# Queries and keys of three attention groups by seven products of halves, with one addition per weight sum

## The chip, the core and the metric

The kernel runs on one core of a Trainium2 chip. The time is the device time of one execution in microseconds (us), measured on the chip; the kernel before took 2248.38, 2249.28 and 2249.44 us in three runs (median 2249.28 us). The smallest change that a measurement of this kernel can tell from none is about 0.2%, some 4.5 us.

The engines are called by short names. PE is the matrix engine, PEld its loading of stationary operands. DVE is the vector engine, ACT the engine for activation functions and scaled copies, POOL the general engine whose queue also issues some transfers, and SP the engine that only issues transfers. Each works through a queue of its own in order, and they wait for each other by semaphores.

## The reference, cut to what matters

Two layers of a transformer over 256 tokens of width 2048, in float32. Each layer is a mixer (differential attention in the first, latent attention in the second), an attention over 256 memory tokens and an MLP with squared ReLU of inner width 8192; each of the three begins with an RMS norm and is added to the residual stream. The change touches the first mixer most, and the MLP a little:

```
def diff_attention(h, wqkv, lam_vecs, subln, wo, cos, sin, lambda_init):
    q, k, v = jnp.split(h @ wqkv, 3, axis=-1)          # h: 256 x 2048, wqkv: 2048 x 6144
    q = partial_rope(q.reshape(B, S, 2 * DA_HEADS, DA_HEAD_DIM), cos, sin, DA_ROT)
    k = partial_rope(k.reshape(B, S, 2 * DA_HEADS, DA_HEAD_DIM), cos, sin, DA_ROT)
    ...
        p = jax.nn.softmax(s, axis=-1)
        a = (p[:, :, 0] - lam * p[:, :, 1]).astype(v.dtype)
        return jnp.einsum('bhqk,bkhd->bqhd', a, v)
    o = rms_norm(o, subln) * (1.0 - lambda_init)
    return o.reshape(B, S, D_MODEL) @ wo

def sq_relu_mlp(h, wup, wdown):
    return jnp.square(jax.nn.relu(h @ wup)) @ wdown
```

## The kernel before

**Arithmetic.** Every float32 operand is split into a high and a low part, and each product is computed as high times high, high times low and low times high: three 128x512 matmuls where one would do. A weight arrives as a raw tile of 1 MB (128x2048: four blocks of 128 inputs by 512 outputs). Per half of it (128x1024), ACT casts the high part `whi` (L193) and DVE subtracts it from the raw values to give `wlo` (L194); PE then does 12 matmuls with the half. A raw tile is called a job below; it has two halves and 24 matmuls, and `matmul_chunk` (L241) does four of them for 512 outputs. Activations are kept transposed, as tiles `unit` with both parts of 512 features by 256 tokens.

**Order of work.** The list `plan` names all jobs in the order in which PE uses them, and `fill` keeps four of them ahead (L205). There are six raw tiles, so SP issues a load when an earlier job has been split, and four buffers each of `whi` and `wlo`, so that splitting runs at most four halves ahead of PE. Between the halves `pump` lets small tasks take their turn on PE (transposes, scores, the steps of an attention), so that the chains of softmax and normalization on DVE, ACT and POOL run while PE does jobs. PE's order is that of the program; the order of the other engines' queues comes from the scheduler of the framework, except where `keep_in_program_order` ties an instruction.

**Differential attention.** It has four groups of two heads with 512 outputs each of query, key and value. `project_diff` (L1157) does the three chunks of a group, twelve jobs: `heads_T` (L461) evacuates queries and keys to a tile `ev` (L443), POOL rotates the first quarter of each head with the tables `cos` and `sin` (`rope`, L446 to L459, six small instructions per 128 tokens), PE transposes the result against `identr` and ACT and DVE split it; `values` (L482) evacuates the values. While the attention of one group (`attend_diff`, L615) takes its turns, PE does the output projection of the group before (four `da_wo` jobs) and the twelve jobs of the next group. DVE's part of an attention are the maxima `nmax`, the reciprocals `rsum`, the weighted differences `a` of two softmaxes (L631, L632), the low parts of transposed probabilities (`raw` from `ax`, L514) and the norm of the heads. The tables are computed once, with a sine on ACT for `sin` (L955) and, after a few DVE steps on the angle that use its result, for `cos` (L959).

**Seven products.** Seven of the eight blocks of each MLP already use a form of Strassen's scheme (class `Seven`, L723): both the tokens and the pair (input half, output half) of the weight are split in two, and seven products p1 to p7 of sums of blocks, two jobs each (x = 0, 1), take the place of eight. Sums of activations s1 to s4 come from class `Forms` (L368). Sums of weights are made in place in the raw tiles: p5 adds a freshly loaded tile to that of p1, and p7 adds the same tile to that of p3, on DVE, in two additions of 128x1024 (L760), each just ahead of the split of that half; p6 and p4 come from tiles to which the next block is added by an accumulating transfer on POOL's queue (L765). Seven's jobs stand between other jobs of the MLP (`pr` are its banks, `mm` those of the others). Sums of products end in 128x512 additions on DVE (L794).

Of the kernel before, what the change touches and what calls it, by code (L numbers as in the profile page):

```python
# [17 lines left out]
P = 128  # L18
# [27 lines left out]
def trunk(ctx, tc, x, xT, mem, memT, positions, gcols, gfinal, lam_vecs, consts, W, out):  # L46
# [321 lines left out]
    class Forms(Stream):  # L368
# [11 lines left out]

        def halves(self, key, x, src):
# [20 lines left out]
        def sums(self):  # L402
# [3 lines left out]
            for x in range(2):  # L406
                a11, a12, a21, a22 = (self.raw[t][:, 8 * h + 4 * x : 8 * h + 4 * x + 4] for t in range(NT) for h in range(2))
                for key, o, p, q, op in (
                    ("s1", a22, a21, a22, ALU.subtract), ("s3", a21, a11, a21, ALU.subtract),
                    ("s2", a22, a22, a11, ALU.subtract), ("s4", a12, a12, a22, ALU.add),  # L410
                ):
                    nc.vector.tensor_tensor(o, p, q, op)
                    self.halves(key, x, o)
                yield T_TURN

# [8 lines left out]
        def unit_of(self, u):  # L424
            return FormUnit(self, u)

# [188 lines left out]
    def attend_diff(q, k, v, dst, coef, subcols):  # L615


        def block(t, heads, out):
# [17 lines left out]
            yield T_TURN  # L636
            if not out:
                out.append((yield from side_bank()))
            po = out[0]
            nb = nk // P  # L640
            for i, h in enumerate(heads):
                for kb in range(nb):
# [3 lines left out]
                        val(v, 0, kb, h * S, S), val(v, 1, kb, h * S, S), kb == 0, kb == nb - 1,  # L646
# [76 lines left out]
    class Seven:  # L723
# [20 lines left out]
        def job(self, p, x):  # L744
            def run():
# [11 lines left out]
                for h in range(2):  # L757
                    if other is not None:
                        half = slice(2 * h * CH, 2 * (h + 1) * CH)
                        nc.vector.tensor_tensor(o[:, half], o[:, half], other[:, half], ALU.add)  # L760
# [13 lines left out]
        def products(self, a, u, copied, out):  # L774
            p, x = u
            form = a.form(self.A[p])
            need(form.tasks)
# [4 lines left out]
            for h, (hi, lo) in enumerate(take()):  # L782
                for k in range(2):
                    kk = 4 * x + 2 * h + k
                    wh, wl = (w[:, k * CH : (k + 1) * CH] for w in (hi, lo))
                    mmul(o, form[:, 0, kk], wh, kk == 0 and not onto, False, not onto)
                    mmul(o, form[:, 0, kk], wl, False, False, not onto)
                    mmul(o, form[:, 1, kk], wh, False, kk == 7, not onto)
# [618 lines left out]
```

## Time and profile before

| | |
|---|---|
| runs before, median | 2249.28 us |
| the profiled execution | 2248.09 us, of which its span is 2246.3 us |
| PE busy | 2221.8 us of the span (99%) |
| DVE busy | 1683.7 us (75%) |
| ACT busy | 1366.9 us (61%) |
| POOL busy | 154.0 us (7%) |
| moved | 484.10 MB, 216 GB/s mean |
| differential attention with its four groups | about the first 360 us |
| the two MLPs' seven products | about 560 to 1080 and 1620 to 2150 us |

The times of the engines are those in which an instruction runs; PE's matmuls overlap, each 128x512 lasts 0.39 us and the next starts before it ends. A row of the timeline has the start in us, the duration in us, engine, line, operation, output and inputs with the buffer numbers left out, shapes and a count; in brackets stands how long the engine had been idle and who ended that. A row of the waits has engine and line, what it waited for, the sum in us, the count and the longest. A row of the windows gives a stretch of time and each engine's busy time in it, the number of its instructions in brackets, then PE's granted clock, the share of the transfer engines and GB/s.

### The profile page before, as it was taken

How to read it: one execution, taken by the hardware profiler on the slowest of the kernel's cores; microseconds unless marked ns; L12 is line 12 of the kernel's file. 1: busy time of each engine (PE TensorE's matmuls, PEld its weight loads, DVE VectorE, ACT ScalarE, POOL GpSimd, SP SyncE). 2: the span in 40 equal slices, each digit the busy share in tenths (PEclk: the TensorE clock that was granted, in tenths of full speed). 3: DMA queues.
4: the chain of work that ended last, by engine and by line, in shares of the span. 5: the costliest groups of instructions: out<-in, count | busy, mean ns of one | idle time of the engine just before them, and what ended most of it. 6: DMA issues, size and time to landing. Idle time of an engine off the chain costs nothing.

```text
span 2246.3 us, 27519 instructions
## 1 busy us (share of the span) xinstructions
PE 2221.8 (99%) x10521; PEld 1853.4 (83%) x10521; DVE 1683.7 (75%) x1892; ACT 1366.9 (61%) x1815; POOL 154.0 (7%) x250
## 2 busy tenths in 40 slices
PE   9999999999999999999999999999999999999998
PEld 7888888888888888888889888888888888888886
DVE  6665647778878788788765766778887887887864
ACT  7544645666666666666655655566666666666664
POOL 0201010000000000000000311000000000000001
PEclk9999999999999999999999999999999999999999
DMA  9446555436887887887955334643689788788682
GB/s 364 168 135 219 193 192 200 162 124 221 245 273 230 243 269 236 243 262 225 282 177 181 111 141 151 243 150 133 238 250 264 237 246 261 238 245 262 231 299 75
DMA packets 73717, 484.10 MB, mean 216 GB/s; under 512 B 8432, under 2 KB 8816, under 8 KB 18032
## 3 DMA queue, kind: packets, MB, share of 16 engines
q1 hardware_dynamic: 64944, 422.56, 52.1%
q0 software_dynamic: 8064, 58.72, 13.7%
q8 instruction: 82, 1.34, 0.2%
q10 hardware_dynamic: 576, 1.05, 0.2%
q14 instruction: 51, 0.42, 0.1%
HBM read 480.20 MB, written 2.10 MB: 215 GB/s over the span
## 4 chain that ended last, share of the span: by engine, by line
PE 92%; DVE 5%; ACT 1%; DMA 0%; issue 0%; ACTq 0%; POOLq 0%
PE mm L155 66%; PE pr L155 21%; PE ax L155 3%; DVE raw L760 2%; DVE wlo L194 2%; PE ax L159 2%; PE mm L159 1%; ACT whi L193 1%; DMA raw<-in_da_wqkv_dram 0%; DVE unit L289 0%; DVE x L438 0%; DVE unit L316 0%; DVE unit L487 0%; DVE os L658 0%; ACT unit L571 0%
## 5 line engine op out<-in xcount | busy, mean ns | idle before, releaser
L194 DVE TENSOR_TENSOR wlo<-raw,whi 128x1024 fp32r<-128x1024 f32 (+2 forms) x962 | 1161.3, 1212 | 470.2 <-ACT whi L193 430.6
L193 ACT CAST whi<-raw 128x1024 fp32r<-128x1024 f32 (+2 forms) x962 | 1002.1, 1042 | 742.9 <-PE mm L155 583.0
L155 PE MATMUL mm<-whi,unit 128*128 128x512 f32 (+3 forms) x4544 | 1442.1, 389 | 1.5 <-ACT unit L571 0.9
L155 PEld LDWEIGHTS mm<-whi,unit 128*128 128x128 f32 x4544 | 849.1, 188 | 168.0 <-ACT unit L315 1.5
L155 PE MATMUL mm<-wlo,unit 128*128 128x512 f32 (+3 forms) x2272 | 877.1, 386 | 11.8 <-DVE wlo L194 11.8
L155 PEld LDWEIGHTS mm<-wlo,unit 128*128 128x128 f32 x2272 | 427.4, 188 | 95.5 <-DVE wlo L194 17.2
L155 PE MATMUL pr<-whi,unit 128*128 128x512 f32 x1568 | 501.9, 390 | 0.0
L155 PEld LDWEIGHTS pr<-whi,unit 128*128 128x128 f32 x1568 | 294.4, 188 | 61.0
L155 PE MATMUL pr<-wlo,unit 128*128 128x512 f32 x784 | 305.0, 389 | 0.0
L155 PEld LDWEIGHTS pr<-wlo,unit 128*128 128x128 f32 x784 | 147.2, 188 | 30.3
L760 DVE TENSOR_TENSOR raw<-raw,raw 128x1024 f32<-128x1024 f32 x112 | 133.5, 1219 | 0.9 <-DMA raw<-in_mlp_wup_dram 0.7
L765 POOL DMA_DIRECT2D raw<-in_mlp_wup_dram x56 | 49.4, 882 | 1126.4 <-DVE wlo L194 1126.4
L438 DVE TENSOR_TENSOR x<-x,mm 128x512 f32<-128x512 f32 x152 | 99.8, 681 | 9.4 <-PE mm L155 8.9
L328 POOL TENSOR_TENSOR rs<-rs,mhalf 128x1 f32<-128x1 f32 (+1 forms) x28 | 23.5, 845 | 679.8 <-DVE rs L327 679.8
L288 ACT CAST unit<-ax 128x512 fp32r<-128x512 f32 (+1 forms) x88 | 49.0, 568 | 26.1 <-PE ax L159 23.6
L289 DVE TENSOR_TENSOR unit<-ax,unit 128x512 fp32r<-128x512 f32 (+1 forms) x88 | 57.4, 661 | 3.4 <-ACT unit L288 1.3
L500 ACT ACTIVATE p<-ax,nmax 128x256 f32<-128x256 f32 (+1 forms) x80 | 33.7, 429 | 30.0 <-DVE nmax L498 29.5
L322 ACT ACTIVATE junk<-x 128x512 bf16<-128x512 f32 x56 | 35.2, 628 | 9.4 <-DVE x L438 8.4
L155 PE MATMUL ax<-unit,unit 128*128 128x256 f32 (+1 forms) x240 | 37.2, 281 | 0.0
L155 PEld LDWEIGHTS ax<-unit,unit 128*128 128x128 f32 x240 | 34.4, 190 | 2.5
L155 PE MATMUL ax<-raw,unit 128*128 128x256 f32 (+1 forms) x240 | 35.3, 279 | 0.8 <-ACT unit L486 0.6
L155 PEld LDWEIGHTS ax<-raw,unit 128*128 128x128 f32 x240 | 32.0, 190 | 2.4 <-ACT unit L486 1.0
(150 smaller groups left out, 925.5 us busy)
## 6 DMA issues: line engine op xcount, KB each, us to landing
raw<-in_mlp_wup_dram SPq DMA_DIRECT2D x128, 1024.0 KB, 5.0
raw<-in_mlp_wdown_dram SPq DMA_DIRECT2D x128, 1024.0 KB, 5.3
raw<-in_mlp_wup_dram POOLq DMA_DIRECT2D x56, 1024.0 KB, 9.5
raw<-in_da_wqkv_dram SPq DMA_DIRECT2D x45, 1024.0 KB, 5.0
raw<-in_da_wo_dram SPq DMA_DIRECT2D x16, 1024.0 KB, 5.0
raw<-in_ca_wkv_dram SPq DMA_DIRECT2D x16, 1024.0 KB, 5.0
raw<-in_mla_wo_dram SPq DMA_DIRECT2D x16, 1024.0 KB, 5.2
raw<-in_ca_wq_dram SPq DMA_DIRECT2D x8, 1024.0 KB, 4.9
```

Of the source, the lines that this page charges most:

```text
L155: return nc.tensor.matmul(o, stationary, moving, start=start, stop=stop, skip_group_check=not alone)
L159: nc.tensor.transpose(o, src, ident)
L193: nc.scalar.copy(hi, r)
L194: nc.vector.tensor_tensor(lo, r, f32(hi), ALU.subtract)
L288: nc.scalar.copy(hi, src)
L289: nc.vector.tensor_tensor(dst[:, 1, :n, t * P : (t + 1) * P], src, f32(hi), ALU.subtract)
L322: nc.scalar.activation(junk[:, : src.shape[1]], src, AF.Square, accum_out=acc)
L328: nc.gpsimd.tensor_tensor(r[:, :n], r[:, :n], mhalf.broadcast_to([P, n]), ALU.pow)
L438: nc.vector.tensor_tensor(xc, xc, ps, ALU.add)
L500: nc.scalar.activation(pr[:, i * w : (i + 1) * w], sb[:, i * w : (i + 1) * w], AF.Exp, bias=nmax[:, i : i + 1], accum_out=ssum[:, i : i + 1],)
L760: nc.vector.tensor_tensor(o[:, half], o[:, half], other[:, half], ALU.add)
L765: add = nc.gpsimd.dma_start(o, self.source(*block, x), accum_op=ALU.add)
```

## The change

**Queries and keys of groups 1, 2 and 3** are computed by `Seven`, which now takes the name of any weight and a first chunk. The two output halves are the 512 queries and the 512 keys of the group, the two input halves are those of the 2048 features, and the two token halves the two tiles of 128 tokens. A job of `Seven` feeds one output bank of 128 tokens, so its half has six matmuls and the job twelve: 14 jobs take the place of the group's eight jobs of 24. Each group's p5 and p7 need four weight sums on DVE and its p6 and p4 four accumulating transfers on POOL's queue.

**The sums of activations** come from the new class `GivenForms`: SP loads the transposed input once more (2 MB, into two raw tiles), ACT multiplies it by the norm's gain, DVE makes the sums and ACT and DVE split them, into four units. This happens once, behind the query chunk of group 0.

**The order of the jobs** is set by `diff_line`: the 14 jobs are laid between eight others, the output projection of the group before (for the first line the values of group 0) and the values of the next group. So the attention of group 0 begins before its own values exist, and it now waits for them (`while not v()`). Rotated queries and keys (`rotated_T`) wait until the attention before has given its units free.

**The weight sums**, in the groups and in the MLPs alike, are now one addition of 128x2048 each (L787), ahead of both splits of the job, and tied to the program's order; before there were two of 128x1024, one ahead of each split, which the scheduler placed. The number of free banks for side tasks is one lower while the lines run.

```diff
+    class GivenForms(Forms):
+        def __init__(self, src, units, gcol):
+            self.src, self.units, self.gcol = src, units, gcol
+            self.forms = {}
+            task = Task(self.sums())
+            for key in ("s1", "s2", "s3", "s4"):
+                self.form(key).tasks.append(task)
+
+        def sums(self):
+            for x in range(2):
+                rows = raw_tile().rearrange("p (k t) -> p k t", t=S)
+                for h in range(2):
+                    u = 2 * h + x
+                    load(rows[:, 4 * h : 4 * h + 4], self.src[:, 4 * u : 4 * u + 4, :])
+                    for i in range(4):
+                        row = rows[:, 4 * h + i]
+                        nc.scalar.activation(row, row, AF.Copy, scale=g[:, self.gcol + 4 * u + i : self.gcol + 4 * u + i + 1])
+                    yield T_TURN
+                self.sums_of(x, *(rows[:, 4 * h : 4 * h + 4, t * P : (t + 1) * P] for t in range(NT) for h in range(2)))
+                yield T_SM
+
+        def pieces(self, key):
+            if key in self.forms:
+                return super().pieces(key)
+            t, h = key
+            return [], lambda half, kk: self.units[2 * h + kk // 4].get(half, kk % 4, t)
 
...
             yield T_TURN
+            while not v():
+                yield 0.5
...
-    plan_k("da_wqkv", 24)
-    for gi in range(1, 4):
-        plan_rows("da_wo", gi - 1)
-        if gi < 3:
-            plan_k("da_wqkv", 12, start=12 * (gi + 1))
-    plan_k("ca_wkv0", 4)
-    plan_rows("da_wo", 3)
...
-        def __init__(self, l, b):
-            self.l, self.b = l, b
+        def __init__(self, name, chunk, b=None):
...
         def source(self, i, j, x):
-            return W[f"mlp_wup{self.l}"][4 * (2 * self.b + j) + 2 * i + x]
+            return W[self.name][4 * (self.chunk + j) + 2 * i + x]
...
                 split = split_pieces(o, 4 * CH, 2)
-                for h in range(2):
-                    if other is not None:
-                        half = slice(2 * h * CH, 2 * (h + 1) * CH)
-                        nc.vector.tensor_tensor(o[:, half], o[:, half], other[:, half], ALU.add)
+                if other is not None:
+                    tc.keep_in_program_order(nc.vector.tensor_tensor(o, o, other, ALU.add))
+                for _ in range(2):
                     split.next()
...
+                    mmul(o, form(0, kk), wh, kk == 0 and not onto, False, not onto)
+                    mmul(o, form(0, kk), wl, False, False, not onto)
+                    mmul(o, form(1, kk), wh, False, kk == 7, not onto)
...
+    def diff_line(gi):
+        values_of = lambda g: [("da_wqkv", 12 * g + 8 + u, CH) for u in range(4)]
+        others = values_of(0) if gi == 0 else [("da_wo", 4 * c + gi - 1, CH) for c in range(4)]
+        others = [Item(None, None, [job]) for job in others + values_of(gi + 1)]
+        seven = Seven("da_wqkv", 3 * (gi + 1)).items()
+        line = []
+        for n in (2, 1, 1, 1, 0, 2, 1) if gi == 0 else (1, 1, 1, 1, 1, 2, 1):
+            line += seven[:2] + others[:n]
+            del seven[:2], others[:n]
+        return line
+
+    diff_lines = [diff_line(gi) for gi in range(3)]
+    plan_k("da_wqkv", 8)
+    for line in diff_lines:
+        plan.extend(j for item in line for j in item.jobs)
+    plan_rows("da_wo", 2)
+    plan_k("ca_wkv0", 4)
+    plan_rows("da_wo", 3)
...
+    def chunk_steps(units_in, finish):
+        n = len(units_in)
+        ps = [bank("mm") for _ in range(NT)]
+        for u, act in enumerate(units_in):
+            need(act.tasks)
+            for h, (hi, lo) in enumerate(take()):
+                for t in range(NT):
+                    unit_part(ps[t], act, h, hi, lo, t, u == 0, u == n - 1)
+            if u == n - 1:
+                finish(ps)
+            yield
+
...
+    def rotated_T(src, r, t, i, dst, free):
+
+
+        nc.scalar.activation(r, src, AF.Copy, scale=da_scales[i][t])
+        rope(r.rearrange("p (h d) -> p h d", h=4), *rotation(t))
+
+        def task():
+            yield T_ROT
+            while not free():
+                yield 0.5
+            b = yield from side_bank()
+            split(dst, t, transpose4(r, b))
+            give_back()
+            yield T_TURN
+
+        dst.run(task())
...
+    q, k = Held(unit()), Held(unit())
+    for i, dst in enumerate((q, k)):
+            heads_T(ps[t], t, lambda i=i, t=t: da_scales[i][t], dst, rotation(t), given=lambda: da_scales)
+        if i == 0:
+            forms = GivenForms(xT, acts, G_ATTN)
+    v, before, copied = [], None, {}
+    free_banks[0] -= 1
+    for gi, line in enumerate(diff_lines):
+        o = attend_group(q, k, v)
+        nq, nk, nv = Held(unit()), Held(unit()), []
+        other = value_steps(v) if gi == 0 else output_steps(before)
+        other_then = value_steps(nv)
+
+        def produced(t, c, src, r, o=o, pair=(nq, nk)):
+            rotated_T(src, r, t, c, pair[c], lambda: all(task.done for task in o.tasks))
+
+        for item in line:
+            if item.of is not None:
+                item.of.products(forms, item.u, copied, produced)
+            elif next(other, 0) == 0:
+                next(other_then)
+        assert next(other_then, 0) == 0
+        if gi == 1:
+            mem_norm()
+        q, k, v, before = nq, nk, nv, o
```

In counts, PE's 128x512 matmuls of the projections fall by 72 (three groups, each from 192 to 168). The sums on DVE change from 112 of 128x1024 to 68 of 128x2048, the splits from 926 to 962, and POOL's queue gets 12 more accumulating transfers of 1 MB.

Three places in the queues follow. The first is ACT's queue at the tables of the rotation, just before the first rotated queries are needed. Before:

```order
L193 CAST whi_414<-raw_412 128x1024
L443 ACTIVATE ev_491<-mm_210,rq_442 128x512
L955 ACT_TABLE_LOAD
L955 ACTIVATE sin<-ang 128x96
L443 ACTIVATE ev_589<-mm_370,r_83_444 128x512
L193 CAST whi_418<-raw_412 128x1024
L443 ACTIVATE ev_601<-mm_371,r_84_446 128x512
L959 ACTIVATE cos<-ang 128x96
```
After, where `raw_563` is the second tile of the input loaded again, `unit_375` to `unit_378` are the four sums, L478 is the evacuation and `p_134_712<-pr_665` copies the first product:

```order
L478 ACTIVATE ev_638<-mm_379,r_87_470 128x512
L478 ACTIVATE ev_650<-mm_380,r_88_472 128x512
L830 COPY p_134_712<-pr_665 128x512
L193 CAST whi_594<-raw_592 128x1024
L193 CAST whi_598<-raw_592 128x1024
L388 CAST unit_375<-raw_563 128x512
L388 CAST unit_377<-raw_563 128x512
L1002 ACT_TABLE_LOAD
L1002 ACTIVATE sin<-ang 128x96
L388 CAST unit_376<-raw_563 128x512
L1006 ACTIVATE cos<-ang 128x96
L388 CAST unit_378<-raw_563 128x512
```
The sine now stands behind the copy of the first product, two casts and two high parts of the sums, and another high part stands between sine and cosine.

The second is DVE's queue in the MLP, from p4's last splits to the first of p5. Before, `wlo_7175` and `wlo_7179` belong to p4, the two tiles of p5 are `raw_7042` (x = 0) and `raw_7077` (x = 1), and `raw_7194` is the job that PE does just before p5:

```order
L194 TENSOR_TENSOR wlo_7175<-raw_6734,whi_7174 128x1024
L760 TENSOR_TENSOR raw_7042<-raw_7042,raw_7220 128x1024 x2
L194 TENSOR_TENSOR wlo_7179<-raw_6734,whi_7178 128x1024
L760 TENSOR_TENSOR raw_7077<-raw_7077,raw_7271 128x1024 x2
L289 TENSOR_TENSOR unit_7125<-ax_7263,unit_7125 128x4x128
L194 TENSOR_TENSOR wlo_7197<-raw_7194,whi_7196 128x1024
L194 TENSOR_TENSOR wlo_7201<-raw_7194,whi_7200 128x1024
L194 TENSOR_TENSOR wlo_7224<-raw_7042,whi_7223 128x1024
L794 TENSOR_TENSOR u_1381_7121<-pr_7270,u_1381_7121 128x512
```
After, at another block of the same kind: p5's tiles are `raw_5294` (x = 0) and `raw_5329` (x = 1), and `raw_5446` is the job just before p5:

```order
L194 TENSOR_TENSOR wlo_5427<-raw_4984,whi_5426 128x1024
L194 TENSOR_TENSOR wlo_5431<-raw_4984,whi_5430 128x1024
L289 TENSOR_TENSOR unit_5377<-ax_5514,unit_5377 128x4x128
L787 TENSOR_TENSOR raw_5329<-raw_5329,raw_5522 128x2048
L194 TENSOR_TENSOR wlo_5449<-raw_5446,whi_5448 128x1024
L194 TENSOR_TENSOR wlo_5453<-raw_5446,whi_5452 128x1024
L787 TENSOR_TENSOR raw_5294<-raw_5294,raw_5472 128x2048
L822 TENSOR_TENSOR u_1105_5373<-pr_5521,u_1105_5373 128x512
L194 TENSOR_TENSOR wlo_5476<-raw_5294,whi_5475 128x1024
```
Before, both sums stand ahead of the splits of the job in front of p5; after, the sum for x = 1 stands ahead of these splits, and that for x = 0 behind them.

The third is DVE's queue in the attention of group 0, from the maximum of the third score tile (`ax_904` before, `ax_984` after) to its weighted difference (`a_922` before, `a_1002` after). Before:

```order
L498 TENSOR_REDUCE nmax_913<-ax_904 128x2
L194 TENSOR_TENSOR wlo_736<-raw_729,whi_735 128x1024
L514 TENSOR_TENSOR raw_927<-ax_807,raw_927 128x256
L505 RECIPROCAL rsum_919<-ssum_914 128x2
L625 TENSOR_TENSOR rsum_919<-rsum_919,coef 128x2
L631 TENSOR_SCALAR a_922<-p_915,rsum_919 128x256
L632 SCALAR_TENSOR_TENSOR a_922<-p_915,rsum_919,a_922 128x256
```
After, the last twelve rows of that way:

```order
L194 TENSOR_TENSOR wlo_921<-raw_797,whi_920 128x1024
L540 RECIPROCAL rsum_999<-ssum_994 128x2
L522 SCALAR_TENSOR_TENSOR unit_1049<-mm_714,r_87_470,unit_1049 128x512
L194 TENSOR_TENSOR wlo_925<-raw_797,whi_924 128x1024
L660 TENSOR_TENSOR rsum_999<-rsum_999,coef 128x2
L522 SCALAR_TENSOR_TENSOR unit_1049<-mm_715,r_88_472,unit_1049 128x512
L549 TENSOR_TENSOR raw_1046<-ax_935,raw_1046 128x256
L194 TENSOR_TENSOR wlo_965<-raw_962,whi_964 128x1024
L666 TENSOR_SCALAR a_1002<-p_995,rsum_999 128x256
L327 TENSOR_SCALAR rs_1083<-ss_205_1078 128x2
L194 TENSOR_TENSOR wlo_969<-raw_962,whi_968 128x1024
L667 SCALAR_TENSOR_TENSOR a_1002<-p_995,rsum_999,a_1002 128x256
```
Before, one split stands between maximum and difference; after, four stand in these twelve rows alone, and with them the evacuation of the values of group 0 (`unit_1049`), which before was done when the attention began.

More of the change, by code (lines that the diff above doesn't have):

```diff
@@ L1177, in trunk @@
+    free_banks[0] += 1
+    o = attend_group(q, k, v)
+    m = []
+    project_group(before, each=lambda c: m.append(given_unit(memT, c, G_MEM)))
+    mk = mem_keys(m)
+    norm = Stream(G_CROSS)
+    project_group(o, norm)
     norm = cross(0, norm, m, mk)
```

64 lines of the change are left out of this document (34 added, 30 removed).

## The prediction

> **What bounds the kernel now.** I read the page first, then the windows over the groups of the differential attention and over an MLP, then what PE waited for, and last the timelines at the places that the change moves. The page's first lines:
>
> ```profile
> span 2246.3 us, 27519 instructions
> PE 2221.8 (99%) x10521; PEld 1853.4 (83%) x10521; DVE 1683.7 (75%) x1892; ACT 1366.9 (61%) x1815; POOL 154.0 (7%) x250
> ```
>
> The profiled execution took 2248.09 us, 1.8 us outside its span, and 1.2 us less than the median of the runs, 2249.28. I make the sum against 2248.1 and add 1.2 at the end. The windows of groups 1 to 3 of the attention and of one MLP stretch (PE, PEld, DVE, ACT, POOL busy):
>
> ```profile
> 82.00:172.00 90.00, 90.00 (x446) 75.76 (x446) 56.64 (x86) 47.34 (x89) 10.84 (x26) 1.00 0.44 152
> 172.00:263.00 91.00, 90.89 (x434) 75.91 (x432) 53.86 (x70) 49.00 (x79) 10.58 (x28) 1.00 0.57 197
> 263.00:354.00 91.00, 91.00 (x434) 76.12 (x433) 54.21 (x68) 44.49 (x68) 9.48 (x26) 1.00 0.54 185
> 700.00:1000.00 300.00, 296.26 (x1327) 243.94 (x1327) 247.66 (x229) 190.24 (x202) 12.31 (x14) 1.00 0.81 247
> ```
>
> PE never stands still in the attention, and DVE has a third of that time free. In the MLP DVE is at 83% and PE loses 1.2%. What PE waited for from 60 to 420 us was one row, and from 420 us to the end almost one cause:
>
> ```profile
> PE ax L159 <- DVE os L658: 0.3, 1, 0.3
> ```
>
> ```profile
> PE mm L155 <- DVE wlo L194: 11.2, 12, 0.9
> ```
>
> So a matmul less is time less, as long as DVE, which the change loads, stays ahead of PE.
>
> **Matmuls removed.** PE in the attention repeats three matmuls (high, low, low) in 0.68 us:
>
> ```profile
> 114.45 0.39 PE L155 MATMUL mm<-wlo,unit 128*128 128x512 f32 x1
> 115.13 0.39 PE L155 MATMUL mm<-wlo,unit 128*128 128x512 f32 x1
> ```
>
> 0.68 / 3 = 0.2275 us a piece; 72 fewer give 16.4 us. They are in the middle of a busy PE, so all of it counts.
>
> **MLP sums.** The twelve waits are one per block, where p5 begins (six of the seven blocks of each MLP). One of them on PE, and DVE's rows ahead of it:
>
> ```profile
> 788.22 0.39 PE L155 MATMUL pr<-whi,unit 128*128 128x512 f32 x1
> 788.45 0.39 PE L155 MATMUL mm<-whi,unit 128*128 128x512 f32 x1
> 789.77 0.50 PE L155 MATMUL mm<-wlo,unit 128*128 128x512 f32 x1 [0.93 <-DVE wlo L194]
> ```
>
> ```profile
> 781.08 1.22 DVE L194 TENSOR_TENSOR wlo<-raw,whi 128x1024 fp32r<-128x1024 f32 x1 [1.17 <-ACT whi L193]
> 782.22 2.35 DVE L760 TENSOR_TENSOR raw<-raw,raw 128x1024 f32<-128x1024 f32 x2
> 784.49 1.22 DVE L194 TENSOR_TENSOR wlo<-raw,whi 128x1024 fp32r<-128x1024 f32 x1
> 785.63 2.35 DVE L760 TENSOR_TENSOR raw<-raw,raw 128x1024 f32<-128x1024 f32 x2
> 787.90 0.68 DVE L289 TENSOR_TENSOR unit<-ax,unit 128x512 fp32r<-128x512 f32 x1
> 788.50 3.48 DVE L194 TENSOR_TENSOR wlo<-raw,whi 128x1024 fp32r<-128x1024 f32 x3
> ```
>
> PE goes on 1.32 us after 788.45 where 0.23 is usual: 1.09 lost, since two pairs of sums (2.35 each) stand ahead of the job's split, which starts at 788.50. In the new order one sum goes ahead and one behind. I replay this block. A sum of 128x2048 is not in the trace; its nearest row is the pair, 2.35, and since pair and following split start 2.27 apart I take 2.25 (bounds 2.1 and 2.4). A split in a row costs (3.48 - 1.22) / 2 = 1.13. The unit's low part waits for its high part on ACT:
>
> ```profile
> 783.67 0.58 ACT L288 CAST unit<-ax 128x512 fp32r<-128x512 f32 x1
> 788.65 1.04 ACT L193 CAST whi<-raw 128x1024 fp32r<-128x1024 f32 x1 [0.26 <-PE pr L155]
> ```
>
> Low part 784.25 to 784.9, sum x=1 to 787.1, two splits to 788.3 and 789.4 (PE wants the first at 788.45 + 0.23 = 788.7), sum x=0 to 791.6, the cast of the sum on ACT 1.05 to 792.7, its split to 793.85. PE wants that after 24 matmuls and one, at 794.1. So both margins are 0.3 to 0.4 us. The sum for x=1 also needs its transfer:
>
> ```profile
> 776.42 3.05 SPq L165 DMA_DIRECT2D raw<-in_mlp_wup_dram  x2
> ```
>
> ```profile
> DMA to landing us min/median/max: 4.7/5.5/13.3
> ```
>
> The second issue of the two ends that row and so starts at 779.1; 5.5 later is 784.6, just before 784.9. I count a third of the blocks late by 0.4, 0.13 on average: 12 x (1.09 - 0.13) = 11.6 us gained; the bounds are 13.1 and nothing.
>
> **Group 0: the tables.** Rows of ACT around sine and cosine, POOL's first rotations, and PE's transposes of them:
>
> ```profile
> 51.70 1.28 ACT L955 ACT_TABLE_LOAD   x1
> 52.99 0.28 ACT L955 ACTIVATE sin<-ang 128x96 f32<-128x96 f32 x1
> 55.27 0.28 ACT L959 ACTIVATE cos<-ang 128x96 f32<-128x96 f32 x1
> ```
>
> ```profile
> 55.62 0.61 POOL L454 TENSOR_TENSOR rope<-ev,cos 128x64 f32<-128x64 f32 x1 [1.59 <-ACT cos L959]
> 58.01 0.32 POOL L454 TENSOR_TENSOR rope<-ev,cos 128x64 f32<-128x64 f32 x1
> 60.81 0.32 POOL L454 TENSOR_TENSOR rope<-ev,cos 128x64 f32<-128x64 f32 x1
> ```
>
> ```profile
> 60.73 1.03 PE L159 MATMUL mm<-identr,ev 128*128 128x128 f32 x8
> ```
>
> After the change the same number of 128x512 matmuls, 241, stands ahead of these transposes, so PE comes to them at 60.7 again. But in ACT's queue the sine now stands behind the copy of product p1, whose last matmul is 12 matmuls, 2.7 us, ahead of the transposes: 58.0. The pieces are the copy, two casts and two high parts, with these rows for the copy and a high part:
>
> ```profile
> 777.76 0.57 ACT L802 COPY p<-pr 128x512 f32<-128x512 f32 x1
> ```
>
> 58.2 + 0.6 + 2 x 0.95 (casts in a row) + 2 x 0.58 = 61.8; table load to 63.1; sine to 63.4; the three DVE steps on the angle, with a sum of forms between them, about 1.1; cosine at 64.5, 9.2 us later than 55.27. POOL then needs 2.4 us for the first and 2.8 for the second tile, as its rows show, and had 0.4 to spare for the second. So PE waits 9.2 - 0.4 = 8.8 us, in two pieces of about 6.4 and 2.4. Nothing hides this: PE's queue is in order, and all attention stands behind.
>
> **Group 0: the attention.** While PE waits, DVE's queue waits too, since the low parts of the transposed queries stand in it. From the end of the second score tile to the transposes of the third difference PE needed this long:
>
> ```profile
> 85.39 0.22 PE L155 MATMUL ax<-maskr,identr 128*128 128x128 f32 x1
> ```
>
> ```profile
> 100.74 0.38 PE L159 MATMUL ax<-identr,a 128*128 128x128 f32 x2
> ```
>
> 15.2 us, with 54 matmuls of 128x512, and 54 stand there after the change. DVE's queue in that stretch then has eight splits (8 x 1.13 = 9.1), a sum (2.25), the pair of values (1.3) and the attention's own instructions (4.5): 17.2, and 0.4 until it can start: 2.4 us late. Group 0 together is 11.2 (6 if half of the tables' delay is made up, 16 at most).
>
> **Groups 1 to 3.** Per group DVE gets 12 splits (13.6), four sums (9.0) and five additions of products (3.0): 54.9 + 25.6 = 80.5 in a group of 90.7 - 5.5 = 85.2. That fits, but with 5 us free where 36 were, and it is late where PE waits for an instruction of the attention behind sums. Where the low part of the probabilities was just in time:
>
> ```profile
> 103.33 0.42 DVE L514 TENSOR_TENSOR raw<-ax,raw 128x256 fp32r<-128x256 f32 x1
> ```
>
> ```profile
> 104.15 0.88 PE L155 MATMUL ax<-unit,raw 128*128 128x256 f32 x6
> ```
>
> it had 0.4 us to spare; in groups 1 and 2 two sums of p7 stand shortly ahead of it, 4.5 us less that 0.4, or 3.9 with what DVE does ahead of time meanwhile. Group 3 has no seven products behind it: 0.3. Together 8.1; the bounds are nothing and two such places per group, 16. The new waits are 11.2 + 8.1 = 19.3 us.
>
> **Taken at nothing:** the second load of the input (2 MB) and 12 MB more of weights, because the transfer engines are at 44 to 57% in the groups (if that cover went, a job would cost its landing, 5.5 against PE's 5.5); the scaling and halving of the sums on ACT, beyond their place ahead of the sine; POOL's 12 issues of 0.9 us beside its 10 us per group; one free bank less (1 us either way).
>
> **Sum.** 2248.1 - 16.4 - 11.6 + 19.3 = 2239.4; with 1.2 for the median, 2240.6 us.
>
> **A rule of the skill.** The warm-up of PE in the trace took 5.45 us for 13 matmuls of 128x512, 0.43 each, against 0.2275 later, and the granted clock in the windows above is 1.00:
>
> ```profile
> 1.23 5.45 PE L905 MATMUL ax<-blank 128*128 128x512 bf16 x13 [1.23 <-DVE blank L902]
> ```
>
> If PE fell back to this after group 0's wait of 6.4 and stayed there as long as at the start, it would lose 5.45 - 13 x 0.2275 = 2.5 us. The Trainium skill ("TensorE: Matmul & The Clock Gate", section "What's actually happening") says that this is what happens after an idle window of about 3.4 us. No wait of PE in the trace, after the start, is over 1.3 us, so no run shows it yet.
>
> **Rivals.**
> - *The clock falls in group 0* as just said: 2243.1. Chance 0.12, given the forecast's waits.
> - *The sums in the MLP only move*: the margins of 0.3 us are gone, because the transfer lands later than 5.5 or the sum takes 2.4, and PE waits another 1.1 somewhere in the block. For it: the longest landing, 13.3, and DVE's 83%. Then -16.4 + 19.3 = +2.9: 2252.2. Chance 0.18.
> - *The cover holds*: DVE uses the wait in group 0 to get ahead, and the rows behind the sums are early: new waits 9, all from the tables. -19: 2230.3. Against it, the order puts sums ahead of rows that are awaited. Chance 0.15.
> - *DVE becomes the bound of the three groups* (slower): of the 36 us per group in which DVE stood idle, mostly for casts that wait for PE to free a buffer, more than 5 remain. Group time is then DVE's 80.5 plus the idle time; the change loses when the groups give back 16.4 + 11.6 + 4.5 - 11.2 = 21.3, 7.1 each, so from 11.8 us idle on. At 14, a group takes 9.3 more: -28.0 + 11.2 + 27.9 = +11.1, or 2260.4. For it: DVE must be ahead of PE but may run only four halves ahead. Against: it was never late before. Chance 0.15.
>
> That the change does less than it says is excluded by PE's queue, which has the 72 matmuls fewer.
>
> **How the numbers follow.** The forecast has 0.40, its own range is 2233 to 2247 (new waits 13 to 26, MLP gain 9 to 13). 0.2% of 2249.3 is 4.5 us, about what a measurement of this kernel can tell; faster means under 2244.8. Faster: 0.34 of the forecast, 0.08 of the clock's case, 0.15 of the cover's: 0.57. Within: 0.06, 0.04 and 0.14 of the sums' case: 0.24. Slower: 0.04 of the sums' case and 0.15 of DVE's: 0.19. For eight in ten I leave out the lower half of the cover's case and the upper half of DVE's: 2230 to 2257.
>
> **What would show it.** Right: PE's row that waits for `wlo` in the MLP shrinks from 11.2 to under 3; a wait of 6 us and one of 2.4 at the transposes near 61 us, cosine near 64.5; PE waits in groups 1 and 2 of a few us for `raw` and `a`; group periods of about 89. Wrong: the twelve MLP waits are still there, or sit elsewhere in the block; no wait at 61 us; a group that takes over 92 us with DVE at over 85; PE's pitch other than 0.2275.

## The result and the profile after

The changed kernel takes 2261.57 us (median of six runs, 2258.68 to 2263.68), the kernel before in the same rounds 2248.98 us: a ratio of 1.0058, 95% interval 1.0047 to 1.0068. It is 12.6 us slower where 8.7 us less was forecast. The profiled execution took 2263.42 us, 1.9 above the median, with a span of 2261.6.

The page's first lines, as for the kernel before:

```profile
span 2261.6 us, 27542 instructions
PE 2218.6 (98%) x10449; PEld 1843.1 (81%) x10449; DVE 1758.3 (78%) x1915; ACT 1402.9 (62%) x1881; POOL 185.1 (8%) x262
```

PE's instructions are 72 fewer, and its busy time hardly falls. The windows of the stretch in which the changed groups lie, and the MLP stretch:

```profile
60.00:120.00 60.00, 46.65 (x218) 38.23 (x216) 48.22 (x68) 38.20 (x66) 13.30 (x27) 0.86 0.47 154
160.00:260.00 100.00, 96.97 (x460) 79.82 (x459) 87.80 (x103) 64.53 (x98) 21.67 (x32) 1.00 0.73 233
260.00:360.00 100.00, 96.50 (x452) 79.79 (x451) 85.52 (x106) 65.74 (x101) 23.41 (x37) 0.98 0.73 234
700.00:1000.00 300.00, 298.66 (x1337) 244.63 (x1336) 247.07 (x218) 190.12 (x210) 10.45 (x12) 1.00 0.75 246
```

PE was fully busy in all of the attention before; now it stands still for 22% of the first row and 3% of the next two, and in the first its granted clock is 0.86. The main rows of what PE waited for up to 420 us, and from there on:

```profile
PE mm L159 <- POOL ev L494: 12.4, 2, 11.8
PE ax L155 <- DVE raw L549: 4.0, 2, 2.2
PE ax L159 <- DVE a L667: 3.0, 2, 2.2
PE mm L155 <- ACT unit L315: 2.9, 2, 1.6
PE pr L155 <- DVE wlo L194: 1.3, 2, 1.0
```

```profile
PE mm L155 <- DVE wlo L194: 3.6, 12, 1.0
PE pr L155 <- DVE wlo L194: 2.8, 4, 0.8
```

The places are those of the forecast; the first is larger, and the MLPs' waits have in part moved from `mm` to `pr`. Two marks in both traces divide the loss: the transposes of the residual behind the attention, and PE's last matmul. Of before:

```profile
417.28 1.04 PE L159 MATMUL mm<-identr,x 128*128 128x128 f32 x8
```

Of after:

```profile
431.51 1.04 PE L159 MATMUL mm<-identr,x 128*128 128x128 f32 x8
```

At this mark after is 14.2 us behind, at the last matmul (2237.10 and 2252.06) 15.0. So the MLPs gave nothing, and all that stands ahead of the first mark lost 14.2 + 16.4 = 30.6 us against the forecast's 19.3.

### The profile page after: what moved, and what is told of

It reads as the page before. It is cut to its first block, busy times and chain, and to the rows that moved or that the text cites. A ratio compares the mean times of both kernels' runs of the same rounds, so it can differ in the third digit from the quotient of the medians.

```text
span 2261.6 us, 27542 instructions
## 1 busy us (share of the span) xinstructions
PE 2218.6 (98%) x10449; PEld 1843.1 (81%) x10449; DVE 1758.3 (78%) x1915; ACT 1402.9 (62%) x1881; POOL 185.1 (8%) x262
## 4 chain that ended last, share of the span: by engine, by line
PE 87%; DVE 7%; ACT 2%; DMA 2%; issue 1%; POOL 1%; ACTq 0%; POOLq 0%; SPq 0%; DVEq 0%
PE mm L155 59%; PE pr L155 23%; DVE wlo L194 3%; PE ax L155 3%; DVE raw L787 2%; PE ax L159 2%; ACT whi L193 2%; PE mm L159 1%; DMA raw<-in_da_wqkv_dram 1%; DMA raw<-in_mlp_wup_dram 1%; DVE unit L289 0%; DVE unit L522 0%; DMA memrow<-in_mem_dram 0%; POOL rope L491 0%; ACT raw L451 0%
## 5 line engine op out<-in xcount | busy, mean ns | idle before, releaser
L194 DVE TENSOR_TENSOR wlo<-raw,whi 128x1024 fp32r<-128x1024 f32 (+3 forms) x998 | 1196.6, 1213 | 421.3 <-ACT whi L193 390.2
L193 ACT CAST whi<-raw 128x1024 fp32r<-128x1024 f32 (+3 forms) x998 | 1030.0, 1041 | 707.3 <-PE mm L155 449.2
L155 PE MATMUL mm<-whi,unit 128*128 128x512 f32 (+3 forms) x4160 | 1327.4, 390 | 3.8 <-ACT unit L315 2.9
L155 PEld LDWEIGHTS mm<-whi,unit 128*128 128x128 f32 x4160 | 780.0, 189 | 156.1 <-ACT unit L315 3.7
L155 PE MATMUL mm<-wlo,unit 128*128 128x512 f32 (+3 forms) x2080 | 805.3, 387 | 3.9 <-DVE wlo L194 3.7
L155 PE MATMUL pr<-whi,unit 128*128 128x512 f32 x1904 | 613.7, 391 | 0.1
L155 PEld LDWEIGHTS mm<-wlo,unit 128*128 128x128 f32 x2080 | 392.6, 189 | 81.6 <-DVE wlo L194 10.0
L155 PEld LDWEIGHTS pr<-whi,unit 128*128 128x128 f32 x1904 | 357.6, 188 | 74.2 <-ACT whi L193 0.8
L155 PE MATMUL pr<-wlo,unit 128*128 128x512 f32 x952 | 373.1, 392 | 4.3 <-DVE wlo L194 4.1
L787 DVE TENSOR_TENSOR raw<-raw,raw 128x2048 f32<-128x2048 f32 x68 | 155.4, 2286 | 1.2 <-DMA raw<-in_mlp_wup_dram 1.2
```

The source lines that it names most:

```text
L155: return nc.tensor.matmul(o, stationary, moving, start=start, stop=stop, skip_group_check=not alone)
L193: nc.scalar.copy(hi, r)
L194: nc.vector.tensor_tensor(lo, r, f32(hi), ALU.subtract)
L787: tc.keep_in_program_order(nc.vector.tensor_tensor(o, o, other, ALU.add))
```

## The experiments

**The MLP sums alone.** The kernel before with:

```
-for h in range(2):
-    if other is not None:
-        half = slice(2 * h * CH, 2 * (h + 1) * CH)
-        nc.vector.tensor_tensor(o[:, half], o[:, half], other[:, half], ALU.add)
-    split.next()
+if other is not None:
+    tc.keep_in_program_order(nc.vector.tensor_tensor(o, o, other, ALU.add))
+for _ in range(2):
+    split.next()
```

> The kernel before with one part of the change: each weight sum of the MLPs is one addition of 128x2048, tied as in the change; the attention is that of before. The prediction's step: 11.6 us less, about 2237.4 us. The theory from the trace after: the tie holds the sum only behind the one DVE instruction traced just before it, the sum for x=1 still goes ahead of the splits of the job in front of p5; each usual block gains 0.43, the first p5 of each MLP loses 1.3 and the last 0.8: 2249 to 2251 us, and PE waits of 0.34 us ahead of p5 where before they were 1.09.

Measured: 2248.01 us against 2248.95, ratio 0.9997 (0.9988 to 1.0005). The 11.6 us are not there; what is left lies within the interval. DVE in the changed kernel, at the start of a p5 whose preceding job PE begins at 803.33, and PE's second matmul of that job:

```profile
798.68 1.23 DVE L194 TENSOR_TENSOR wlo<-raw,whi 128x1024 fp32r<-128x1024 f32 x1 [1.50 <-ACT whi L193]
799.83 0.68 DVE L289 TENSOR_TENSOR unit<-ax,unit 128x512 fp32r<-128x512 f32 x1
800.42 2.28 DVE L787 TENSOR_TENSOR raw<-raw,raw 128x2048 f32<-128x2048 f32 x1
802.63 2.35 DVE L194 TENSOR_TENSOR wlo<-raw,whi 128x1024 fp32r<-128x1024 f32 x2
```

```profile
803.90 0.50 PE L155 MATMUL mm<-wlo,unit 128*128 128x512 f32 x1 [0.18 <-DVE wlo L194]
```

The split of the first row, p4's second, waits 1.50 us for its cast, and the sum behind it ends 0.6 us ahead of the job, where my replay had 1.35. PE waits for the split of 802.63: 0.57 us lie between the two matmuls where 0.23 is usual.

**The sums behind the splits.** The order is what the tie does not fix: it holds a sum behind the one DVE instruction traced just before it (here the low part of a unit), not behind the splits traced earlier, and so the scheduler still puts the sum for x = 1 ahead of the splits of the job in front. In this kernel each half sum is queued behind the last split; `behind_split` ties it to that instruction:

```
+for h in range(2):
+    half = slice(2 * h * CH, 2 * (h + 1) * CH)
+    behind_split(nc.vector.tensor_tensor(o[:, half], o[:, half], other[:, half], ALU.add))
```

> The changed kernel with the weight sums in two halves of 128x1024 again, both queued on DVE behind the last split traced before them, in MLPs and groups alike, which the tie of the change does not do. Theory: PE's waits ahead of p5 in the MLPs come from a sum that stands ahead of the splits of the job in front; here none does, and 10 to 13 us go in the MLPs; in the groups the order changes too, by 3 us either way: 2246 to 2254 us. Rival: DVE is too full there in any order, the waits move to the second job of p5: within 3 us of the changed kernel, 2259 to 2264 us.

Measured: 2258.35 us (1.0042, 1.0029 to 1.0054), 3.2 less than the changed kernel, which the intervals do not separate, and outside both expectations. The trace divides it: at the mark behind the attention this run stands at 436.21, 4.7 behind the changed kernel; from there to the end it gains 10.7 on the kernel before (18.9 behind at the mark, 8.2 at the end of its span of 2254.5). The MLP part is as expected; in the groups the order is worse.

The MLP part alone, in the kernel before:

> The kernel before with one edit: in the MLPs the two half sums of a job are queued on DVE behind the last split traced before them (attention as before). Theory: the order of sums and splits alone is worth 10.8 us there, as the trace of the run with both edits has it from the first MLP to the end: 2236.5 to 2240 us. Rival: that gain needs the changed attention (another phase of the loads) and is not there in the kernel before: 2246 to 2250 us.

Measured: 2238.01 us against 2248.51, ratio 0.9955 (0.9941 to 0.9968): the best kernel of this study, 10.5 us ahead of the kernel before. Its DVE queue at the same block:

```profile
785.57 1.23 DVE L203 TENSOR_TENSOR wlo<-raw,whi 128x1024 fp32r<-128x1024 f32 x1
786.95 1.23 DVE L203 TENSOR_TENSOR wlo<-raw,whi 128x1024 fp32r<-128x1024 f32 x1 [0.16 <-ACT whi L202]
788.10 2.35 DVE L769 TENSOR_TENSOR raw<-raw,raw 128x1024 f32<-128x1024 f32 x2
```

and its window, with PE at 300.00 of 300:

```profile
700.00:1000.00 300.00, 300.00 (x1344) 247.10 (x1343) 249.49 (x233) 189.35 (x204) 12.33 (x14) 1.00 0.77 246
```

DVE's work is the same as before (249 against 248); the order alone was the matter.

**The tables early.** `tables()` moves from `first_norm` to the second job's hook, and its two small loads behind the constants:

```
+def first_loads():
+    load(const, consts)
+    load(pos, positions)
+    load(lamv, lam_vecs)
+def tables_and_x():
+    tables()
+    x_pieces(0, 1)
+hooks[1] = first_loads
+hooks[2] = tables_and_x
```

> The changed kernel with positions and lambda vectors loaded behind the constants, and the tables of sine and cosine computed about 25 us earlier. Theory: most of the 12.9 us that PE waits at the first rotated queries is the tables' place in ACT's queue; then that wait falls to under 4 us (the evacuation of the second query tile is still late in ACT's queue), PE keeps its clock, and the time falls by 12 to 17 us, to 2245 to 2250 us. Rival: ACT's queue as a whole is late there and another instruction in it takes the sine's place: a wait of over 8 us stays and the gain is under 6 us, over 2255 us.

Measured: 2259.15 us (1.0046, 1.0032 to 1.0059), 2.4 less, a difference within the intervals. The theory was right on the wait and wrong on the time. What PE waited for up to 420 us:

```profile
PE ax L159 <- DVE a L667: 4.9, 2, 4.0
...
PE pr L155 <- DVE wlo L194: 3.1, 4, 1.3
PE pr L155 <- ACT whi L193: 3.0, 2, 2.6
PE mm L159 <- POOL ev L494: 1.7, 1, 1.7
```

12.4 us at the transposes became 1.7, but PE then waits for both halves of split weights in the first line (`whi` and `wlo`, from 76 us on) and longer for a difference of softmaxes. The tables were only the first in the queue to be late.

**The sums of activations later**, behind the key chunk (`if i == 1` in place of `if i == 0`):

> The changed kernel with the sums of activations begun behind the key chunk of group 0 in place of the query chunk. Theory: from 42 to 70 us ACT's queue is full with 24 instructions for these sums, and rotation tables and second evacuation come late for that; now they come ahead, the wait of 12.9 us at the transposes goes, and 3 to 7 us come back at p5 of group 0, which waits for its sums: 2250 to 2256 us. Rival: DVE's and ACT's work in group 0 is too much in whatever order, and as much is lost at p5 as was gained: 2258 to 2263 us.

Measured: 2267.62 us (1.0085, 1.0071 to 1.0099), 6 more than the changed kernel, worse than either expectation. The tables are early in this run, and yet the second query tile comes late. POOL and, in the second fence, DVE at that time:

```profile
62.93 1.30 POOL L494 TENSOR_TENSOR ev<-rope,rope 128x64 f32<-128x64 f32 x1
64.19 2.37 POOL L489 TENSOR_TENSOR rope<-ev,cos 128x64 f32<-128x64 f32 x1
66.52 0.77 POOL L490 TENSOR_TENSOR rope<-ev,sin 128x64 f32<-128x64 f32 x1
```

```profile
61.48 2.57 DVE L194 TENSOR_TENSOR wlo<-raw,whi 128x1024 fp32r<-128x1024 f32 x2 [0.53 <-ACT whi L193]
63.97 2.40 DVE L787 TENSOR_TENSOR raw<-raw,raw 128x2048 f32<-128x2048 f32 x1
66.30 1.54 DVE L419 TENSOR_TENSOR raw<-raw 128x512 f32<-128x512 f32 x2
```

A rotation's instruction, 0.32 us where DVE is idle, takes about as long as the DVE instruction beside it: 1.30 beside a split, 2.37 beside a sum, 0.77 beside a sum of activations. (The Trainium skill, "SBUF — State Buffer", section "Terms", describes a pair of ports between DVE and POOL as "Lock-allocated, exclusive, held for the full instruction"; these rows agree.) So a full DVE queue slows the rotations too, which come between the queries and their transposes.

**Without the sums of activations:**

```
-task = Task(self.sums())
-for key in ("s1", "s2", "s3", "s4"):
-    self.form(key).tasks.append(task)
+t, h = {"s1": (1, 1), "s2": (1, 0), "s3": (0, 1), "s4": (0, 0)}.get(key, key)
```

> The changed kernel without the sums of activations: the four loads, 16 scalings, eight sums and their halves are left out, and the products take plain pieces of the activations in their place, so PE's and the weights' work is the same and queries and keys of groups 1 to 3 are not those of the reference. Theory: ACT's and DVE's work for these sums is what PE waits for in group 0; the wait at the transposes (12.9 us), the one at the third difference (2.4 us) and the slow clock behind them (3 us) go, 13 to 18 us: 2244 to 2249 us. Rival: the weight sums and splits of the first line alone keep DVE behind, more than half of it stays at p5 and in the attention of group 0: 2253 us or more.

Measured: 2251.02 us against 2249.17 (1.0007, 0.9998 to 1.0016), 10.5 less than the changed kernel, between the two expectations. Even with this work left out, three groups of seven products gain nothing. Of the wait at the transposes 3.6 us stay, POOL's:

```profile
61.53 1.31 POOL L484 TENSOR_TENSOR rope<-ev,cos 128x64 f32<-128x64 f32 x1
...
65.32 2.37 POOL L487 TENSOR_TENSOR rope<-ev,sin 128x64 f32<-128x64 f32 x1
```

DVE has four splits in a row from 60.03 and a sum from 65.11; from 60.27 on POOL gets one instruction in beside each.

**The wait filled with matmuls:**

```
+for _ in range(46):
+    nc.tensor.matmul(b, acts[0][:, 0, 0, :P], acts[0][:, 0, :2, :], start=True, stop=True)
 split(dst, t, transpose4(e, b))
```

> The changed kernel with 46 matmuls of 128x512 without use on PE just ahead of the first transposes of rotated queries, where PE waits for about 12 us; they go into a bank that the transposes overwrite. They take 46 x 0.2275 = 10.5 us of the wait. Theory of the clock: PE's clock falls because it idles; with these the matmuls behind the wait go at 0.23 us at once instead of 0.43, the end of the wait stays, and the time falls by 3 to 4 us, to about 2258 us. Rival: the slow matmuls behind the wait have another cause (their operands): the spacing of 0.43 us stays, and the time is that of the changed kernel, 2261.6 us, or more.

Measured: 2262.27 us (1.0061, 1.0048 to 1.0073), no gain. PE just behind the extra matmuls:

```profile
72.21 0.66 PE L159 MATMUL mm<-identr,ev 128*128 128x128 f32 x4 [1.36 <-POOL ev L494]
73.99 0.66 PE L159 MATMUL mm<-identr,ev 128*128 128x128 f32 x4 [1.13 <-POOL ev L494]
...
75.08 1.05 PE L155 MATMUL mm<-whi,unit 128*128 128x512 f32 x2
```

The four transposes at 72.21 take 0.66 us, where the same four take 1.11 in the changed kernel, and the granted clock stays 1.00 up to 74.78, where the changed kernel has 0.50 from 65.31 to 82.37. So far the theory is right: PE's idleness, and not the operands, makes the matmuls slow. But two rests of 1.36 and 1.13 us were left, and matmuls behind them are slow again (clock 0.50 from 74.78 to 78.19). Two more such stretches of 3.41 us, from 119.15 and 204.49, stand behind waits for DVE that the changed kernel has too and passed at 1.00. In all PE works 10.2 us at half its clock here between 60 and 420 us, and 10.6 in the changed kernel, so nothing was gained.

**Rests made on purpose**, in the latent attention of the kernel before, where PE never rests:

```
+w = work.tile([P, CH], F32, tag="ev", name=nm("hold"), bufs=EVS)
+nc.scalar.copy(w, ps[0])
+for _ in range((0, 1, 2, 4)[gi]):
+    nc.gpsimd.tensor_tensor(w, w, w, ALU.mult)
+flip(ps[0][:, :P], w[:, :P])
```

> The kernel before with three idle stretches of PE made on purpose in the latent attention, where PE never idles: behind the values of groups 1, 2 and 3 a transpose without use waits for a copy on ACT and for one, two and four additions' worth of POOL (128x512, about 1.5 us each), so about 3, 4.5 and 8 us. Theory from the traces of the changed kernel and of the runs with early tables and the filled wait: PE's clock falls for some 3 us also behind waits of 2 to 3 us, so slow matmuls (0.43 us apart) follow all three, 1.5 to 3 us lost each. Rival, the page's window of about 3.4 us of idleness: none behind the first, some behind the other two. Together 18 to 24 us more than before: 2267 to 2273 us.

Measured: 2270.49 us (1.0098, 1.0082 to 1.0114), 21 more and in the expected range. The rests are 14.6 us in sum:

```profile
PE mm L159 <- POOL hold L1284: 14.6, 3, 6.7
```

Slow matmuls follow all three, as the theory has it, the first rest of 3.4 us included. Against the same matmuls of the kernel before, the stretches behind the rests lose 3.3, 1.7 and 1.5 us, no more behind 6.7 us than behind 3.4. The granted clock is 0.50 for 6.8 us behind the first rest and for 3.4 behind the second; the third such stretch, of 6.8, is in part the rest itself. Behind the middle rest, and the clock behind the first:

```profile
1354.83 0.33 PE L159 MATMUL mm<-identr,hold 128*128 128x128 f32 x1 [4.49 <-POOL hold L1284]
...
1355.46 1.00 PE L155 MATMUL mm<-whi,unit 128*128 128x512 f32 x2
```

```profile
1294.07:1300.89 6.82, 6.82 (x27) 6.24 (x27) 1.05 (x3) 1.50 (x8) 0.00 (x0) 0.50 0.00 0
```

**Fewer groups.** Seven products in groups 2 and 3 only, with the MLPs' sums behind the splits; the lines of the plan become `diff_line(1)` and `diff_line(2)`, and the sums of activations are made during group 1:

```
+before = attend_group(q, k, v)
+forms = GivenForms(xT, acts, G_ATTN)
+q, k, v = project_diff()
```

> Seven products for queries and keys of groups 2 and 3 only; group 1 as in the kernel before, the sums of activations made during it; in the MLPs the half sums behind splits as in the run of that name. Theory: without group 0's part, each of the two groups saves 5.5 us of matmuls and pays the 3.7 to 4.4 us of waits and about 1 us of slow clock that its counterpart shows in the trace after; with 10.8 us of the MLPs: 2234 to 2240 us, within 2 us of the run with the MLP edit alone. Rival: making the sums of activations costs as much anywhere, 8 us or more: 2244 us or more.

Measured: 2240.57 us (0.9964, 0.9952 to 0.9977), just over the expected range and 2.6 behind the kernel with the MLP edit alone, a difference within the intervals; no gain of the two groups is seen. With the groups' sums in two halves, as the scheduler places them:

> As the run with seven products in groups 2 and 3 and the MLPs' half sums behind splits, but with the groups' weight sums in two halves of 128x1024 that the scheduler places, as the kernel before has them in its MLPs. Theory: what stands ahead of an awaited instruction of the attention is then a piece of 1.2 in place of 2.3 us, and POOL's rotations are held up for half as long; the two groups' waits fall from 11 to 6 to 8 us: 2235 to 2238 us. Rival: DVE's total is what counts, not the pieces: 2239 to 2242 us as with whole sums.

Measured: 2238.76 us (0.9955, 0.9942 to 0.9968), 1.8 less than with whole sums and level with the MLP edit alone; between the two expectations, and the difference is no larger than the intervals.

**Both edits to the changed kernel:**

> The changed kernel with the tables early and, in the MLPs, the half sums behind splits. Theory: the two are in different stages and add up: 2259.2 - 10.8, 2246.5 to 2250 us. Rival: they do not add, since the phase of the loads into the MLP shifts with the attention: over 2252 us.

Measured: 2246.77 us (0.9990, 0.9981 to 0.9999), in the expected range. They add up: 12.4 less than with the tables alone, where the MLP edit gave 10.5 by itself.

## Why the prediction was wrong

The sum gave 2239.4 us for a profiled execution, which took 2263.42. Of these 24.0 us the MLP sums are 12.4, the clock 4.5, the tables and the rotation 3.6 and a later start 1.9.

- **Matmuls removed, 16.4 us: right.** The spacing is the same, and PE has the 72 fewer.
- **MLP sums, 11.6 us gained: wrong, the largest error.** Alone they give 0.9 us, within the noise. The step that failed is the replay: I let the second split of p4 start right behind the first. Its cast cannot, since it needs a buffer of `whi` that PE frees (the 1.50 us above). The row stands in the trace of before as well, just ahead of the unit's cast that I used:

```profile
782.72 1.05 ACT L193 CAST whi<-raw 128x1024 fp32r<-128x1024 f32 x1 [1.67 <-PE mm L155]
```

  With it the replay has that split end at 785.0, and the unit's low part start there and not at 784.25. So sum and awaited split came 0.7 us later than I had it, and the margin of 0.3 to 0.4 was a wait of 0.34; p5's second split loses another 0.3 in the same way. The two add up to 7.7 us over twelve blocks, where I had 1.6. The rest is in blocks that I did not replay: the first p5 and the last block of each MLP, where PE did not wait before, now lose about 1 us each (matmul by matmul, the run with the MLP sums alone against the kernel before). It is nearly the rival "the sums in the MLP only move", which I had at 0.18; its cause was not the transfer but that buffer. And I read the order of the queues rightly without asking why x = 1 stood first: a sum behind its splits gives the 10.5 us.
- **Tables and rotation, 8.8 us: place right, 12.4 in size.** I let ACT's queue come to the sine when the first product was done, at 58.2. ACT of the changed kernel:

```profile
59.23 2.50 ACT L451 ACTIVATE raw<-raw,g 128x256 f32<-128x256 f32 x6
63.35 0.57 ACT L830 COPY p<-pr 128x512 f32<-128x512 f32 x1
68.16 0.28 ACT L1002 ACTIVATE sin<-ang 128x96 f32<-128x96 f32 x1
70.02 0.28 ACT L1006 ACTIVATE cos<-ang 128x96 f32<-128x96 f32 x1
```

  The copy is at 63.35, because the scalings ahead of it had filled the queue: ACT works without a rest from 56.00 on, 3.4 us of it at the scalings of L451. I had added only what stands between product and sine. POOL's first tile then took 4.1 us in place of 2.4, with 2.36 of it beside a weight sum.
- **Third difference, 2.4 us: right** (a wait of 2.24 and a slower start). **Groups 1 to 3, 8.1 us: right in size, in part by luck.** The waits for `raw` stand where I had them, behind two sums, but are 1.78 and 2.23 us in place of 3.9 each. What makes up for it had no term of its own: 0.8 for `a`, 1.5 for `wlo`, and 1 to 2 in slower starts. DVE's added work was right: from 60 us to the first mark, before and after, DVE is busy for 80.8 us more, where I had 3 x 25.6 = 76.8, and some of the sums of activations fall into it too:

```profile
60.00:417.28 357.28, 356.82 (x1728) 298.61 (x1728) 228.53 (x317) 192.66 (x321) 37.70 (x95) 1.00 0.53 183
60.00:431.51 371.51, 350.19 (x1666) 289.88 (x1664) 309.34 (x398) 237.81 (x378) 73.16 (x118) 0.97 0.68 221
```

  My rival of DVE as the bound lies at 2260.4, near the result, but not for its reason: the groups' waits are those of the forecast and not 9 us each.
- **The clock, taken at nothing: wrong.** Twelve matmuls behind the transposes go 0.43 us apart, 2.4 us, the eight transposes take 0.9 longer, and six more matmuls behind 300.8 lose 1.2: 4.5 us. The rival of 2.5 us at 0.12 happened in addition to the forecast, not in its place, so the chances should have been given to sums of these causes.

```profile
76.30 1.11 PE L159 MATMUL mm<-identr,ev 128*128 128x128 f32 x4 [0.67 <-POOL ev L494]
...
78.06 1.05 PE L155 MATMUL mm<-whi,unit 128*128 128x512 f32 x2
```

- **The start** is 1.9 us later in this profiled execution (PE comes to the wait at 62.6, before at 60.7). It is not the change's: the run with the MLP sums alone, whose program is that of before up to the first MLP, shows it too:

```profile
9.71 0.50 PE L155 MATMUL mm<-whi,unit 128*128 128x512 f32 x1 [1.76 <-ACT unit L315]
```

In sum, for the profiled execution: -16.4 + 0.8 (MLPs) + 12.4 + 2.4 + 7.5 (groups 1 to 3, with their starts) + 4.5 + 1.9 = 13.1, of 15.3 us in the span; the other 2 us I have not assigned. The common cause of the attention's part is shown by the runs that move its pieces: group 0 has no room in ACT's and DVE's queues for sums of activations and weight sums together (10.5 us come back when the former are left out), and the two later groups cost about what they save (the runs with fewer groups). That POOL's slower rotation is DVE's doing is read from rows that end together in three runs; no run takes DVE's work away from beside it alone.

## What to carry to other kernels

A tie behind the last instruction traced is not program order: look in the queue at which awaited instruction still stands behind the one that was tied. Replaying a queue by hand, start each instruction only when its buffer is free, and count a queue from its last idle moment, not from the operand that one instruction waits for. Taking work from PE pays only where the engines that feed it have room at that very place; here DVE's third of free time was an average, and at the places above the new work stood ahead of an instruction that PE waited for.

## What the runs showed of the hardware

- PE's granted clock falls behind rests well under 4 us, and the length of a rest does not decide it alone. Of two rests of the same length in the changed kernel only the second has slow matmuls behind it (0.58 us for a 128x256):

```profile
121.31 0.44 PE L159 MATMUL ax<-identr,a 128*128 128x128 f32 x2 [2.24 <-DVE a L667]
300.84 0.58 PE L155 MATMUL ax<-unit,raw 128*128 128x256 f32 x1 [2.23 <-DVE raw L549]
```

  In every trace here the clock changes only at steps of a fixed grid of 3.41 us: it is 0.50 for one step from 300.83, for five (17.07 us) from 65.31, and for two behind the first rest made on purpose. The steps around the two rests:

```profile
116.50:119.91 3.41, 2.57 (x17) 2.11 (x15) 3.41 (x8) 2.81 (x6) 0.96 (x2) 1.00 0.98 199
119.92:123.33 3.41, 2.02 (x10) 1.72 (x11) 2.45 (x4) 0.53 (x2) 1.52 (x1) 1.00 1.00 298
297.41:300.82 3.41, 1.19 (x7) 0.83 (x5) 3.37 (x4) 0.94 (x1) 0.00 (x0) 1.00 0.63 216
300.83:304.24 3.41, 3.40 (x10) 2.92 (x11) 3.04 (x4) 2.41 (x7) 0.51 (x1) 0.50 1.03 406
```

  The first rest is divided between two steps, in which PE still works for 2.57 and 2.02 us; the second lies in one, in which PE works for 1.19. In the thirteen traces, between 20 and 2200 us, every step at 1.00 with PE idle for 0.58 of it or more is followed by a step at 0.50, and none with PE idle for less than 0.50 of it is; from 0.50 to 0.53 both happen. (The Trainium skill, "TensorE: Matmul & The Clock Gate", section "What's actually happening", has the clock fall after an idle window of about 3.4 us; the length of the window agrees with the steps, but it need not be idle throughout.)
- An instruction of POOL on 128x64 takes 0.32 us alone and about as long as the DVE instruction with two inputs in memory beside it, 1.30 or 2.37 us; in these rows POOL advances by one instruction per DVE instruction.
- A DVE addition of 128x2048 takes 2.28 us and one of 128x1024 1.22, or 2.35 a pair: the larger form saves nothing to speak of.
